# Router logits of a decoder block with the router's weights as the stationary operand, in two column halves that one further product adds and turns back

## The chip, the cores and the metric

The kernel runs on one NeuronCore of a Trainium2 chip. The metric is the device time of one execution in microseconds (us). Engines are called as the profile calls them: PE is TensorE's matmul, PEld its weight load, DVE VectorE, ACT ScalarE, POOL GpSimd, SP SyncE, whose queue issues most DMAs.

## The reference, cut to what matters

One decoder layer on 1024 tokens of width 1024: adaLN, one input projection, sliding-window attention beside a gated MLP, a merge, a residual, a second adaLN, and a mixture of 32 experts in 4 groups of 8. The change sits in the router of that mixture:

```python
hf = h.reshape(T, D)                                   # T = 1024 tokens, D = 1024
lg = (hf @ w_rg).astype(jnp.float32) + b_rg            # 4 group logits
g_idx = jnp.argmax(lg, axis=-1)                        # best group
le = ((hf @ w_re).astype(jnp.float32) + b_re).reshape(T, N_GROUPS, EXPERTS_PER_GROUP)
le = jnp.take_along_axis(le, g_idx[:, None, None], axis=1)[:, 0]
top_p, top_i = lax.top_k(jax.nn.softmax(le, axis=-1), TOP_K)   # two experts of that group
...
out = jax.ops.segment_sum(yr * row_w[:, None], row_tok, num_segments=T)   # experts on gathered tokens
```

## The kernel before, in words

The program has two parts. The first works on two halves of 512 tokens (`half(0)`, `half(1)`): projections, attention, the gated MLP and the merge, and after each half the product with `w_o` (`wo_stream(0)`, then `wo_pass` for the second half), which makes the residual `X1`. Nearly every large product there is three matmuls (`mm3`, L135 to L137): weights and activations are split into a rounded high part (cast on ACT, L451) and the rest (subtraction on DVE, L452). The second part runs the experts: their weights (2 MB each, `big` tiles, seven buffers) stream from HBM by SP's queue (L1391), and small expert blocks multiply 32 or 64 token columns as stationary operand (L1504).

The router stands between the parts. It works on eight tiles of 128 tokens, t = 0 to 7, with 40 columns of weights `wr` (4 groups, 4 unused, 32 experts):

- `r_setup` (L845) folds the modulation into `wr` (L850) and the bias `brt`.
- `r_pre` (L864, POOL) and `r_store` (L924 on DVE, L925 and L926 as POOL's DMAs) make the normalized tile and write it to HBM, from where the experts gather rows.
- `r_tr` (L852) transposes the tile in eight matmuls (L857) into two PSUM banks, and ACT copies each half to `h2T` (L858).
- `r_logit` (L872) multiplies: for each of eight blocks k of the contraction, the stationary operand is `h2T[:, k]` (128 x 128) and the moving one `wr[:, k]` (128 x 40); the sum stands in one bank `ps`, tokens on partitions (L876). Each such f32 matmul is two PE instructions and two loads in the trace. DVE then finds the best group and the two best experts (L878 to L897).
- `r_rank` (L900) counts, with three small matmuls (L903 to L906), how many earlier tokens chose the same expert; the last of them waits for DVE's choice `Mb` (L896). `tab_tok` (L942) makes from it the list of tokens, and from that POOL gathers the first expert's rows (L1416).

Tiles 0 to 3 are hooked into the jobs of `half(1)` (L1276), tiles 4 to 7 into the last pass of `w_o` (L1325, L1327). Within a queue the order is not the source's: the scheduler of the framework lays out each engine's instructions when the kernel is built, and each engine then works its list in order, waiting at the head. PSUM has eight banks in one pool (`bank()`); four of them hold the query sums of `half(1)` while tiles 0 to 3 pass.

Of the kernel before, what the change touches and what calls it, by code (L numbers as in the profile page):

```python
# [10 lines left out]
F32 = mybir.dt.float32  # L11
# [5 lines left out]
OP = mybir.AluOpType  # L17
AX = mybir.AxisListType

P = 128  # L20
# [81 lines left out]
def block_kernel(ctx: ExitStack, tc: tile.TileContext, x, c, positions, rel_bias, w_ada, b_ada,  # L102
# [6 lines left out]
    PE, DVE, ACT, POOL, SP = nc.tensor, nc.vector, nc.scalar, nc.gpsimd, nc.sync  # L109
# [11 lines left out]
    def nm(s):  # L121
        uid[0] += 1
        return f"{s}_{uid[0]}"
# [4 lines left out]
    def bank(shape=(512,)):  # L128
        return psum.tile([P] + list(shape), F32, name=nm("ps"), tag="ps")
# [17 lines left out]
    ident = keep.tile([P, P], F32, name="ident")  # L147
# [66 lines left out]
    pc = p1.enter_context(tc.tile_pool(name="p1c", bufs=1))  # L214
    hl = p1.enter_context(tc.tile_pool(name="p1hl", bufs=4))
    xw = p1.enter_context(tc.tile_pool(name="p1xw", bufs=5))
    sm = p1.enter_context(tc.tile_pool(name="p1sm", bufs=2))
# [604 lines left out]
        return j  # L822


    wr = pc.tile([P, 8, 40], F32, name="wr")
    brt = pc.tile([P, 40], F32, name="brt")
    sh2c = pc.tile([P, 8], F32, name="sh2c")
    g2c = pc.tile([P, 8], F32, name="g2c")
    DVE.memset(wr[:, :, 4:8], 0.0)
    DVE.memset(brt[:, 4:8], NEG)  # L830
    cum = keep.tile([P, 2, NE], BF16, name="cum")

# [12 lines left out]
    def r_setup():  # L845
        ps = bank()
        for k in range(8):
            PE.matmul(ps[:, 0:40], sh2c[:, k:k + 1].to_broadcast([P, P]), wr[:, k], start=(k == 0), stop=(k == 7))
        DVE.tensor_tensor(brt, ps[:, 0:40], brt, op=OP.add)
        DVE.tensor_tensor(wr, wr, g2c.unsqueeze(2).to_broadcast([P, 8, 40]), op=OP.mult)  # L850

    def r_tr(t, n):  # L852
        if n == 0:
# [17 lines left out]

    def r_logit(t):  # L872
        h2T = R.pop(("T", t))
        ps = bank()
        for k in range(8):
            PE.matmul(ps[:, 0:40], h2T[:, k], wr[:, k], start=(k == 0), stop=(k == 7))  # L876
        lg = sm.tile([P, 40], F32, name=nm("lg"), tag="lg")
        DVE.scalar_tensor_tensor(lg, ps[:, 0:40], R["rs", t], brt, op0=OP.mult, op1=OP.add)  # L878
        gm = sm.tile([P, 8], F32, name=nm("gm"), tag="gm")
        gi = sm.tile([P, 8], U32, name=nm("gi"), tag="gi")  # L880
        DVE.max(gm, lg[:, 0:8])
        DVE.max_index(gi, gm, lg[:, 0:8])
        pen = sm.tile([P, 4], F32, name=nm("pen"), tag="pen")
        DVE.tensor_tensor(pen, iota_u[:, 0:4], gi[:, 0:1].to_broadcast([P, 4]), op=OP.not_equal)
        le = sm.tile([P, 4, 8], F32, name=nm("le"), tag="le")
        DVE.scalar_tensor_tensor(le, pen.unsqueeze(2).to_broadcast([P, 4, 8]), NEG,
                                 lg[:, 8:40].rearrange("p (g e) -> p g e", g=4), op0=OP.mult, op1=OP.add)
        lef = le.rearrange("p a b -> p (a b)")
        ei = sm.tile([P, 8], U32, name=nm("ei"), tag="ei")
        DVE.max(mx8[:, t], lef)  # L890
        DVE.max_index(ei, mx8[:, t], lef)
        oh = sm.tile([P, 2, NE], F32, name=nm("oh"), tag="oh")
        DVE.tensor_tensor(oh, iota_u.unsqueeze(1).to_broadcast([P, 2, NE]),
                          ei[:, 0:2].unsqueeze(2).to_broadcast([P, 2, NE]), op=OP.is_equal)
        Mb = sm.tile([P, NE], BF16, name=nm("Mb"), tag="Mb")
        DVE.tensor_tensor(Mb, oh[:, 0], oh[:, 1], op=OP.add)  # L896
        DVE.tensor_scalar(lgs[:, t], lg[:, 0:4], gm[:, 0:1], None, op0=OP.subtract)  # L897
        R["oh", t] = (oh, Mb)
# [277 lines left out]
    def wo_stream(h):  # L1176
# [7 lines left out]
        for n in range(2):  # L1184
# [24 lines left out]
            jobs.hook(idx[-1], ev)  # L1209
            jm = jobs.add(*m)  # L1210
        jobs.hook(jm, lambda: (rows_load((1, 2)), r_setup()))
        return idx

# [60 lines left out]
    for t in range(4):  # L1274
        both = lambda fn: lambda t: (fn(t, 0), fn(t, 1))
        for d, fn in ((0, both(r_pre)), (0, r_sq), (0, both(r_tr)), (1, r_store), (2, r_logit), (4, r_rank)):  # L1276
            jobs.hook(q0 + 2 * t + d, lambda fn=fn, t=t: fn(t))
# [46 lines left out]
    for i, at in ((4, (1, 2, 4, 5, 7)), (5, (2, 3, 5, 6, 8))):  # L1324
        for j, fn in zip(at, (lambda t: r_tr(t, 1), r_logit, r_rank, tab_tok, r_store)):  # L1325
            jobs.hook(w2[j], lambda fn=fn, i=i: fn(i))
    for fn in (lambda t: r_tr(t, 1), r_store, r_logit, r_rank, tab_tok):  # L1327
        for i in (6, 7):
            jobs.hook(w2[-1], lambda fn=fn, i=i: fn(i))
# [439 lines left out]
    def table(t, cols, n):  # L1769
        if t == 0:  # L1770
            R["rest"] = bank()
        ps = R["rest"][:, 0:2 * n]
        tmp = wk.tile([P, D], F32, name=nm("y"), tag="y")
        A, C = (tmp[:, o:o + 2 * m].rearrange("p (k r) -> p k r", k=2) for o, m in ((0, P), (2 * P, n)))
        V = tmp[:, HT:HT + 4 * n].rearrange("p (k a n) -> p k a n", k=2, a=2)
        one_hots(A, C, t, cols)
        POOL.tensor_tensor(V[:, :, 0], C, wts[:, t].unsqueeze(2).to_broadcast([P, 2, n]), op=OP.mult)
        POOL.tensor_tensor(V[:, :, 1], C, pay[:, t].unsqueeze(2).to_broadcast([P, 2, n]), op=OP.mult)
        for k in range(2):
            PE.matmul(ps, A[:, k], V[:, k].rearrange("p a b -> p (a b)"), start=(t == 0 and k == 0),  # L1780
                      stop=(t == 7 and k == 1))
        return ps.rearrange("p (a n) -> p a n", a=2)
# [141 lines left out]
    with tc.If(nover > 0):  # L1924
# [32 lines left out]
        for t in range(8):  # L1957
            ps = table(t, cols[:, 0:NO], NO)
# [4 lines left out]
        with tc.For_i(0, nover, 1) as s:  # L1963
# [15 lines left out]
            for z, key in ((0, "g"), (1, "u")):  # L1979
                PS[X, key] = bank()  # L1980
                for kk in range(0, 8, 2):
                    wh, wl = split2(raws[z][:, kk:kk + 2])
                    for q in range(2):
                        k = kk + q
# [31 lines left out]
def build(inputs):  # L2016
    import concourse.bacc as _bacc

    nc = _bacc.Bacc("TRN2", target_bir_lowering=False, num_devices=1)
    arrays, args = {}, []  # L2020
    for name in _INS:
        a = np.ascontiguousarray(inputs[name])
        arrays[f"in_{name}_dram"] = a
        args.append(nc.dram_tensor(f"in_{name}_dram", a.shape, mybir.dt.from_np(a.dtype), kind="ExternalInput").ap())
    for i, (shape, dtype) in enumerate(_OUTS):
        dt = mybir.dt.from_np(np.dtype(dtype))
        args.append(nc.dram_tensor(f"out_{i}_dram", shape, dt, kind="ExternalOutput").ap())
    with tile.TileContext(nc) as tc:
        block_kernel(tc, *args)
    return nc, arrays  # L2030
# [8 lines left out]
```

## Time and profile before

| | us |
|---|---|
| median of 3 runs | 1276.06 (1275.82 to 1279.53) |
| the profiled execution | 1274.85 |
| its span, first to last instruction | 1273.2 |
| PE busy in the span | 1147.2 (90%) |
| DVE busy | 772.3 (61%) |
| ACT busy | 555.3 (44%) |
| POOL busy | 221.0 (17%) |
| mean granted clock of TensorE | 0.951 |

All sums below are made against the profiled execution; 1274.85 lies 1.21 under the median. Times within the program are us from the span's start. Busy shares are averages over stages with different limits, so the stretches around the router are what to read. A granted clock of 1.00 is 2.4 GHz, 0.50 is 1.2 GHz.

### The profile page before, as it was taken

How to read it: one execution, taken by the hardware profiler on the slowest of the kernel's cores; microseconds unless marked ns; L12 is line 12 of the kernel's file. 1: busy time of each engine (PE TensorE's matmuls, PEld its weight loads, DVE VectorE, ACT ScalarE, POOL GpSimd, SP SyncE). 2: the span in 40 equal slices, each digit the busy share in tenths (PEclk: the TensorE clock that was granted, in tenths of full speed). 3: DMA queues.
4: the chain of work that ended last, by engine and by line, in shares of the span. 5: the costliest groups of instructions: out<-in, count | busy, mean ns of one | idle time of the engine just before them, and what ended most of it. 6: DMA issues, size and time to landing. Idle time of an engine off the chain costs nothing. (4 is left out here: it accounts for less than half of the span.)

```text
span 1273.2 us, 18583 instructions
## 1 busy us (share of the span) xinstructions
PE 1147.2 (90%) x6873; PEld 878.1 (69%) x6874; DVE 772.3 (61%) x1698; ACT 555.3 (44%) x970; POOL 221.0 (17%) x325
## 2 busy tenths in 40 slices
PE   5899999999989999899996998998999998899851
PEld 3788887778878988688774665665665656676530
DVE  7668885567767888444497455664425635695015
ACT  4459742335525784233242244543414424673021
POOL 3500010111041000010034211121022121112201
PEclk9999999999989999899995999899999998999975
DMA  9734436547354345523856999999889999999994
GB/s 318 227 103 125 133 114 217 182 158 255 114 185 150 124 133 182 170 85 106 350 200 215 409 401 415 402 381 402 330 299 405 380 324 411 414 360 363 401 409 162
DMA packets 106345, 334.70 MB, mean 263 GB/s; under 512 B 7998, under 2 KB 52158, under 8 KB 81800
## 3 DMA queue, kind: packets, MB, share of 16 engines
q1 hardware_dynamic: 92438, 296.66, 61.6%
q0 software_dynamic: 13712, 36.77, 10.0%
q8 instruction: 55, 0.90, 0.3%
q14 instruction: 42, 0.34, 0.1%
q10 hardware_dynamic: 98, 0.03, 0.0%
HBM read 314.54 MB, written 25.71 MB: 267 GB/s over the span
## 5 line engine op out<-in xcount | busy, mean ns | idle before, releaser
L135 PE MATMUL ps<-big,hi 128*128 128x512 f32 x544 | 220.2, 405 | 9.7 <-ACT hi L451 9.4
L452 DVE TENSOR_TENSOR lo<-big,hi 128x1024 fp32r<-128x1024 f32 x156 | 185.5, 1221 | 67.1 <-ACT hi L451 66.3
L136 PE MATMUL ps<-big,hi 128*128 128x512 f32 x544 | 216.5, 398 | 4.1 <-DVE big L452 4.0
L137 PE MATMUL ps<-big,lo 128*128 128x512 f32 x544 | 215.7, 397 | 0.0
L451 ACT CAST hi<-st 128x512 fp32r<-128x512 f32 x192 | 116.2, 619 | 205.7 <-PE ps L136 117.4
L452 DVE TENSOR_TENSOR lo<-st,hi 128x512 fp32r<-128x512 f32 x192 | 135.3, 715 | 107.1 <-ACT hi L451 106.6
L451 ACT CAST hi<-big 128x1024 fp32r<-128x1024 f32 x156 | 159.4, 1050 | 69.1 <-PE ps L137 68.5
L1504 PE MATMUL ps<-big,xTh 128*32 128x128 f32 (+1 forms) x1792 | 133.4, 337 | 8.0 <-DMA big<-in_w_gate_dram 3.3
L135 PEld LDWEIGHTS ps<-big,hi 128*128 128x128 f32 x544 | 105.0, 193 | 33.4 <-ACT hi L451 11.1
L136 PEld LDWEIGHTS ps<-big,hi 128*128 128x128 f32 x544 | 104.9, 193 | 29.1 <-DVE big L452 5.9
L137 PEld LDWEIGHTS ps<-big,lo 128*128 128x128 f32 x544 | 104.5, 192 | 23.1 <-DVE lo L452 0.9
L1504 PEld LDWEIGHTS ps<-big,xTh 128*32 128x32 f32 (+1 forms) x1792 | 83.3, 126 | 48.7 <-issue 17.1
L136 PE MATMUL ps<-lo,xTh 128*128 128x512 f32 x224 | 94.2, 420 | 12.8 <-DVE lo L452 12.6
L135 PE MATMUL ps<-hi,xTh 128*128 128x512 f32 x224 | 94.2, 421 | 11.2 <-ACT hi L451 11.2
L137 PE MATMUL ps<-hi,xTl 128*128 128x512 f32 x224 | 91.3, 408 | 0.0
L135 PE MATMUL ps<-hi,big 128*128 128x256 f32 (+1 forms) x256 | 88.4, 346 | 0.1
L136 PE MATMUL ps<-lo,big 128*128 128x256 f32 (+1 forms) x256 | 86.8, 339 | 1.1 <-DVE lo L452 1.1
L137 PE MATMUL ps<-hi,big 128*128 128x256 f32 (+1 forms) x256 | 86.5, 338 | 0.0
L1421 POOL DMA_INDIRECT zd<-y,rows_i x30 | 50.8, 1695 | 175.3 <-DVE y L1581 96.1
L1416 POOL DMA_INDIRECT xg<-h2d,rows_i x30 | 36.2, 1207 | 220.9 <-PE ps L1448 101.5
L1504 PE MATMUL ps<-big,aTh 128*32 128x256 f32 (+1 forms) x448 | 64.3, 513 | 5.4 <-DMA big<-in_w_down_dram 5.4
L1577 DVE SCALAR_TENSOR_TENSOR y<-ps,w_sb,g 128x512 f32<-128x512 f32 (+1 forms) x20 | 12.9, 643 | 91.1 <-PE ps L1504 84.0
(382 smaller groups left out, 1865.5 us busy)
## 6 DMA issues: line engine op xcount, KB each, us to landing
big<-in_w_gate_dram SPq DMA_DIRECT2D x32, 2048.0 KB
big<-in_w_up_dram SPq DMA_DIRECT2D x32, 2048.0 KB
big<-in_w_down_dram SPq DMA_DIRECT2D x30, 2048.0 KB
st<-in_w_in_dram SPq DMA_DIRECT2D x26, 1024.0 KB
st<-in_w_ada_dram SPq DMA_DIRECT2D x16, 1024.0 KB
st<-in_w_o_dram SPq DMA_DIRECT2D x10, 1024.0 KB
big<-in_x_dram SPq DMA_DIRECT2D x16, 512.0 KB
bias<-biasd POOLq DMA_DIRECT2D x16, 512.0 KB
```

The costliest lines, as they stand in the source:

```text
L135: PE.matmul(ps, lh, rh, start=start, stop=False)
L136: PE.matmul(ps, lh, rl, start=False, stop=False)
L137: PE.matmul(ps, ll, rh, start=False, stop=stop)
L451: ACT.copy(hi, src)
L452: return DVE.tensor_tensor(lo, src, f(hi), op=OP.subtract)
L1416: return POOL.indirect_dma_start(out=t[0:n, 0:D // q], out_offset=None, in_=in_parts(src, q), in_offset=bass.IndirectOffsetOnAxis(ap=idx[0 ...
L1421: return POOL.indirect_dma_start(out=in_parts(dst, q), out_offset=bass.IndirectOffsetOnAxis(ap=idx, axis=0), in_=t[:, 0:D // q], in_offset ...
L1504: PE.matmul(ps[n * e:n * e + n, 0:m], xt[:, s * i:s * i + n], cols_w, start=start, stop=stop)
L1577: DVE.scalar_tensor_tensor(y, ps[:, 0:D // q], w, G2p[q], op0=OP.mult, op1=OP.mult)
```

## The change

`wr` gets 64 columns instead of 40, the last 24 of them zero. For block k the stationary operand is now `wr[:, k]` (128 x 64), the moving one `h2T[:, k]` (128 x 128 tokens). Even blocks sum into partitions 0 to 63 of a bank `pt`, odd ones into 64 to 127, so that matmuls of the two column halves of the array alternate. ACT copies the bank to `lT` (L882 of the changed kernel), and one more product (L884) with `f40`, two stacked 40-column identities, adds the halves and brings tokens back to partitions. `lT` takes its buffers from the tag `tA` of `tab_tok`, and each tile now takes two banks.

```diff
-    wr = pc.tile([P, 8, 40], F32, name="wr")
+    wr = pc.tile([P, 8, 64], F32, name="wr")
...
     DVE.memset(wr[:, :, 4:8], 0.0)
+    DVE.memset(wr[:, :, 40:64], 0.0)
+    f40 = pc.tile([P, 40], F32, name="f40")
+    DVE.tensor_tensor(f40, ident[:, 0:40], ident[:, 64:104], op=OP.add)
...
-            PE.matmul(ps[:, 0:40], sh2c[:, k:k + 1].to_broadcast([P, P]), wr[:, k], start=(k == 0), stop=(k == 7))
+            PE.matmul(ps[:, 0:40], sh2c[:, k:k + 1].to_broadcast([P, P]), wr[:, k, 0:40], start=(k == 0), stop=(k == 7))
         DVE.tensor_tensor(brt, ps[:, 0:40], brt, op=OP.add)
-        DVE.tensor_tensor(wr, wr, g2c.unsqueeze(2).to_broadcast([P, 8, 40]), op=OP.mult)
+        DVE.tensor_tensor(wr, wr, g2c.unsqueeze(2).to_broadcast([P, 8, 64]), op=OP.mult)
...
     def r_logit(t):
         h2T = R.pop(("T", t))
+
+        pt, lT = bank(), sm.tile([P, P], F32, name=nm("lT"), tag="tA")
+        for k in range(0, 8, 2):
+            for h in range(2):
+                PE.matmul(pt[64 * h:64 * h + 64, 0:P], wr[:, k + h], h2T[:, k + h], start=(k == 0), stop=(k == 6))
+        ACT.copy(lT, pt[:, 0:P])
         ps = bank()
-        for k in range(8):
-            PE.matmul(ps[:, 0:40], h2T[:, k], wr[:, k], start=(k == 0), stop=(k == 7))
+        PE.matmul(ps[:, 0:40], lT, f40, start=True, stop=True)
```

Lines after the edit move by 3 to 8: L857 becomes L860, L864 L867, L903 to L906 become L911 to L914, L925 becomes L933.

The scheduler also lays out other instructions anew. On PE at tiles 1 and 2, before (`ps_4408` is tile 1's logits, `ps_4452` and `ps_4458` are tile 2's transposes, `ps_4396` is tile 0's rank):

```order
L876 MATMUL ps_4408<-wr,h2T_4346 128x40 x4
L857 MATMUL ps_4452<-ident,big_3718 128x128
L876 MATMUL ps_4408<-wr,h2T_4346 128x40 x4
L857 MATMUL ps_4452<-ident,big_3718 128x128 x3
L857 MATMUL ps_4458<-ident,big_3718 128x128 x4
L135 MATMUL ps_4223<-big_3781,hi_4287 128x512
...
L135 MATMUL ps_4224<-big_3781,hi_4287 128x512
L906 LDWEIGHTS tri_b
L906 MATMUL ps_4396<-Mb_4327,tri_b 128x32
```

The same place now (`ps_4415` and `ps_4426` are tile 1's two products, `ps_4463` and `ps_4469` tile 2's transposes, `ps_4403` tile 0's rank):

```order
L881 MATMUL ps_4415<-h2T_4353,wr 64x128 x8
L137 MATMUL ps_4226<-big_3784,lo_4291 128x512
L135 MATMUL ps_4227<-big_3784,hi_4290 128x512
L884 MATMUL ps_4426<-f_187,lT_4416 128x40
L860 MATMUL ps_4463<-ident,big_3721 128x128
L914 LDWEIGHTS tri_b
L914 MATMUL ps_4403<-Mb_4334,tri_b 128x32
L860 MATMUL ps_4463<-ident,big_3721 128x128 x3
L860 MATMUL ps_4469<-ident,big_3721 128x128 x4
L136 MATMUL ps_4227<-big_3785,hi_4290 128x512
```

The rank product of tile 0 now stands after one of tile 2's eight transposes instead of after all eight; the number of 512-column matmuls ahead of it is the same (eight since tile 0's logits began to be due), and fourteen follow it before the next rank product in either order.

On POOL around the same tiles, before (`h_548` to `h_616` are tiles 0 to 3):

```order
L864 TENSOR_TENSOR h_548_4237<-big_3718,rc_4204 128x512 x2
L864 TENSOR_TENSOR h_568_4330<-big_3718,rc_4204 128x512 x2
L864 TENSOR_TENSOR h_592_4435<-big_3718,rc_4204 128x512
L925 DMA h2d<-h_548_4237 128x1024
L925 DMA h2d<-h_568_4330 128x1024
L864 TENSOR_TENSOR h_592_4435<-big_3718,rc_4204 128x512
L864 TENSOR_TENSOR h_616_4541<-big_3718,rc_4204 128x512 x2
```

And now:

```order
L867 TENSOR_TENSOR h_548_4240<-big_3721,rc_4207 128x512 x2
L867 TENSOR_TENSOR h_570_4337<-big_3721,rc_4207 128x512 x2
L933 DMA h2d<-h_548_4240 128x1024
L933 DMA h2d<-h_570_4337 128x1024
L867 TENSOR_TENSOR h_596_4446<-big_3721,rc_4207 128x512 x2
L867 TENSOR_TENSOR h_622_4556<-big_3721,rc_4207 128x512 x2
```

The fifth of the eight multiplications moved behind the two DMAs, so four stand in a row there instead of three.

On PE at the end of the router, tiles 6 and 7, before:

```order
L857 MATMUL ps_7281<-ident,big_6663 128x128 x4
L876 MATMUL ps_7293<-wr,h2T_7143 128x40 x8
L876 MATMUL ps_7320<-wr,h2T_7202 128x40 x8
L903 LDWEIGHTS ones_b
L903 MATMUL ps_7347<-ebase,ones_b 128x32
```

And now:

```order
L860 MATMUL ps_7308<-ident,big_6682 128x128 x4
L881 MATMUL ps_7320<-h2T_7170,wr 64x128 x8
L884 MATMUL ps_7331<-f_187,lT_7321 128x40
L881 MATMUL ps_7351<-h2T_7229,wr 64x128 x8
L884 MATMUL ps_7362<-f_187,lT_7352 128x40
L911 LDWEIGHTS ones_b
```

Each turning product follows its own tile's logits directly, with nothing between the two.

## Rows read from the trace of the kernel before

**Rows 1.** Busy time by stretch (us from the span's start). Columns: stretch, its length, then busy us and instruction count of PE, PEld, DVE, ACT and POOL, the granted clock, the DMA engines' busy share, GB/s.
```profile
340.00:400.00 60.00, 56.02 (x292) 47.35 (x291) 43.91 (x159) 20.11 (x38) 18.59 (x21) 0.91 0.48 160
368.00:373.00 5.00, 5.00 (x25) 5.00 (x26) 3.66 (x6) 0.57 (x1) 4.12 (x5) 0.50 0.37 147
400.00:520.00 120.00, 117.50 (x688) 103.05 (x686) 95.66 (x291) 75.67 (x175) 9.13 (x19) 1.00 0.47 153
640.00:671.00 31.00, 27.81 (x157) 21.64 (x156) 29.22 (x97) 12.99 (x28) 10.35 (x12) 1.00 0.64 228
671.00:690.00 19.00, 10.74 (x59) 9.88 (x59) 17.00 (x101) 3.53 (x7) 7.41 (x12) 0.50 0.75 265
690.00:700.00 10.00, 9.36 (x89) 5.37 (x93) 4.61 (x20) 3.80 (x6) 5.20 (x12) 0.50 0.35 105
700.00:980.00 280.00, 260.24 (x1607) 176.84 (x1598) 139.31 (x183) 106.72 (x139) 51.35 (x47) 0.98 0.98 382
```

**Rows 2.** All instructions of the logits' line: duration of one in ns (least, median, most), start of the first and the last, form.
```profile
L876 PEld LDWEIGHTS ps<-wr,h2T x128: 187/192/370, 362.5 to 678.3; 128*128 128x128 f32 x128
L876 PE MATMUL ps<-wr,h2T x128: 197/283/415, 362.7 to 678.3; 128*128 128x40 f32 x128
```

**Rows 3.** Order of time on PE and PEld around tile 5's logits: start, us taken by the row, engine, line, operation, count.
```profile
655.33 0.40 PE L137 MATMUL ps<-hi,big 128*128 128x512 f32 x1
655.33 1.99 PEld L876 LDWEIGHTS ps<-wr,h2T 128*128 128x128 f32 x16
655.56 1.87 PE L876 MATMUL ps<-wr,h2T 128*128 128x40 f32 x16
657.26 0.47 PE L135 MATMUL ps<-hi,big 128*128 128x512 f32 x1
```

**Rows 4.** The same view in the experts' part, where the stationary operand has 64 columns (`128*64`) or 32: full-width loads ahead of 64-column ones, those, and a full-width load after 32-column matmuls.
```profile
752.47 1.15 PEld L1458 LDWEIGHTS ps<-ident,xg 128*128 128x128 f32 x8
753.74 3.22 PEld L1504 LDWEIGHTS ps<-big,xTh 128*64 128x64 f32 x32
753.74 3.67 PE L1504 MATMUL ps<-big,xTh 128*64 128x256 f32 x32
703.50 0.14 PEld L1552 LDWEIGHTS ps<-ident,sl 128*128 128x128 f32 x1 [0.20 <-issue]
```

**Rows 5.** A matmul, ACT's copy of its result, and a load that waits for such a copy (order of time; in brackets the idle time before, and what ended it).
```profile
703.50 0.33 PE L1552 MATMUL ps<-ident,sl 128*128 128x128 f32 x1
703.86 0.27 ACT L1554 COPY aTh<-ps 128x128 f32<-128x128 f32 x1 [4.03 <-PE ps L1552]
690.01 0.59 ACT L1449 COPY xTh<-ps 128x512 f32<-128x512 f32 x1 [1.78 <-PE ps L1448]
690.64 1.48 PEld L1504 LDWEIGHTS ps<-big,xTh 128*32 128x32 f32 x32 [1.12 <-ACT xTh L1449]
```

**Rows 6.** PE in order of time at tiles 1 and 2.
```profile
365.46 0.50 PE L137 MATMUL ps<-big,lo 128*128 128x512 f32 x1
367.95 1.90 PE L876 MATMUL ps<-wr,h2T 128*128 128x40 f32 x8 [1.99 <-DVE lg L878]
371.46 1.74 PE L857 MATMUL ps<-ident,big 128*128 128x128 f32 x7
377.28 0.18 PE L906 MATMUL ps<-Mb,tri_b 128*128 128x32 bf16 x1 [1.99 <-DVE Mb L896]
377.31 0.59 PE L136 MATMUL ps<-big,hi 128*128 128x512 f32 x1
382.28 0.18 PE L903 MATMUL ps<-ebase,ones_b 1*128 1x32 bf16 x1
```

**Rows 7.** DVE and POOL in order of time at the same tiles.
```profile
368.80 2.27 DVE L924 SCALAR_TENSOR_TENSOR h<-h,rs,rb 128x1024 f32<-128x1024 f32 x1 [0.99 <-POOL h L864]
372.02 3.70 DVE L897 TENSOR_SCALAR lgs<-lg,gm 128x4 f32<-128x4 f32 x1
377.05 0.18 DVE L896 TENSOR_TENSOR Mb<-oh 128x32 bf16<-128x32 f32 x1
364.05 5.94 POOL L864 TENSOR_TENSOR h<-big,rc 128x512 f32<-128x512 f32 x4
371.93 3.75 POOL L864 TENSOR_TENSOR h<-big,rc 128x512 f32<-128x512 f32 x3
```

**Rows 8.** The end of the router in order of time: logits of tiles 6 and 7 on PE, their first reader on DVE (tile 7's), a DVE row beside POOL's memsets, the list of tokens, and the next weight load of SP's queue after 667.8.
```profile
671.86 6.89 PE L876 MATMUL ps<-wr,h2T 128*128 128x40 f32 x32
678.79 0.26 DVE L878 SCALAR_TENSOR_TENSOR lg<-ps,rs,brt 128x40 f32<-128x40 f32 x1 [0.62 <-PE ps L876]
680.43 1.30 POOL L1657 MEMSET z<- 128x512 f32 x4
680.64 1.11 DVE L913 CAST si<-sf 128x2 int32<-128x2 f32 x1
684.81 0.16 DVE L939 SCALAR_TENSOR_TENSOR tok_s<-tS,tk 128x4 int32<-128x4 f32 x1
698.21 0.38 SPq L1391 DMA_DIRECT2D big<-in_w_up_dram  x1
```

**Rows 9.** The scaling of `wr` in `r_setup`, and DVE's first wait of the program.
```profile
L850 DVE TENSOR_TENSOR wr<-wr,g2c x1: 482/482/482, 350.3 to 350.3; 128x320 f32<-128x320 f32 x1
7.09 0.21 DVE L313 COPY ccol<-ps 128x48 f32<-128x48 f32 x1 [3.93 <-PE ps L312]
```

## The prediction

> **What bounds the kernel now.** I read the busy time by stretch first, because the change touches two short windows. It shows [rows 1] three regimes. From 400 to 520, PE is busy 117.50 of 120 us: work taken from PE, or put on it, before that moves everything behind it. From 640 to 671, DVE is busy 29.22 of 31 and PE 27.81, so there DVE sets the pace. From 671 to 690 the clock is 0.50, PE is mostly idle, and a chain runs through PE and DVE to the list of tokens. From 700 on, the DMA engines are busy 0.98 of the time at 382 GB/s: the experts' part is a stream of weights. That stream stands at 0.35 between 690 and 700, since its buffers come free only when the first expert has multiplied; SP issues the next load at 698.21 [rows 8]. So the experts' end moves with the end of the router nearly one for one. The second view is order of time in the two windows. At tiles 1 and 2 it shows PE waiting twice, 1.99 us for tile 0's reader of the logits and 1.99 for tile 0's `Mb` [rows 6]; both times DVE is late because POOL multiplies beside it: L897 took 3.70 us, and it began and ended with POOL's three L864 [rows 7]. At tiles 6 and 7, PE does the logits in one piece of 6.89 us from 671.86, and DVE waits 0.62 for the last [rows 8].
>
> **What a tile's logits cost, before and after.** Before: 128 matmuls in eight tiles are 16 each [rows 2]. Tile 5's sixteen start at 655.56 and the next matmul starts at 657.26: 1.70 us, 0.106 each [rows 3]. A 40-column matmul is not what takes that long; the loads of 128 columns come at this pace (16 in 1.99 with the last one's length) [rows 3]. At the low clock it is 6.89/32 = 0.215 [rows 8].
>
> After: a load has 64 columns, a matmul 128 moving columns. The nearest rows are the experts' with 64-column stationary operands and 256 moving ones: 32 in 3.67 us, and less the last one's overhang of about 0.25 that is 0.107 each, while 32 loads take 3.22 [rows 4]. Half the moving columns make 0.053, and loads of 64 at half the pace of 128 [rows 3] are 0.053 too. Sixteen take 0.86 at the full clock, 1.72 at the low one. The bounds are 0.053 and the 0.106 of now; I take the lower since those rows have the same pattern of halves. The Trainium skill (TensorE: Matmul & The Clock Gate, Part 3: Packing small matmuls) has a rule against this: a load overlaps matmuls in flight only where the row groups differ, and here only column groups differ. By that rule a tile would cost 16 x (0.053 + 0.107) = 2.56, by the rows 0.86; the rows bear against it, since 64-column loads and matmuls run side by side there [rows 4].
>
> Going into and out of the half-width form costs something: a full-width load after narrow matmuls stood idle 0.20 [rows 4], and the first 64-column load starts at 753.74, 0.12 after the last full-width one ended (752.47 + 1.15), with its matmul at the same instant instead of 0.23 behind [rows 3, 4]. I take 0.2 each way, 0.4 a tile (0 to 0.6). The turning product is two more full-width loads, 0.21 (0.43 at the low clock). So a tile at the full clock goes from 1.70 to 0.86 + 0.4 + 0.21 = 1.47: **0.23 less**, not the half that the columns suggest.
>
> The product waits for ACT's copy. From a 128-column matmul's start to the copy is 0.36, of which 0.11 is its own columns; the copy takes 0.27; a load follows a copy's end by 0.04 [rows 5]. That is 0.25 + 0.27 + 0.04 = 0.56. At tiles 0 to 5, two or three 512-column matmuls (0.23 each, 655.33 to 655.56 [rows 3]) stand between, 0.45 and more, and with the change of form (0.2) that covers it. At tiles 6 and 7 nothing stands between and the wait is bare.
>
> **The sum.** *Tiles 0 and 1* gain nothing: PE waits behind them for DVE anyway, and tile 1's product waits for tile 0's reader as its logits did. *Tiles 2 to 5*: 4 x 0.23 = -0.9, but the new order breaks into the logits of tiles 2 and 4 with another matmul, two more changes there and back, +0.8; together **-0.1** (-3.8 if all of tiles 0 to 5 kept 0.63 each, with no change of form; +1.5 if each product waits 0.4). *Tile 0's rank product* now stands ahead of seven transposes of tile 2. `Mb` comes when POOL lets DVE go: before, POOL's last three ended at 375.68 and `Mb` came at 377.05 [rows 7]. Now four stand in a row, but can start earlier, since L924 of tile 1, at 368.80, no longer runs beside a fifth (2.27 us with it) [rows 7]; the one makes up for the other and I keep 377.3. The seven transposes, formerly done before the wait, come after it: 1.74 at the low clock, some 1.5 at the 0.215 pace. The fourteen matmuls after them, 4.97 us from 377.31 to 382.28 [rows 6], then start later and more of them at the full clock, 0.7 back: **+0.8** (-0.3 to +3.4). *Tiles 6 and 7*: each 0.2 + 1.72 + 0.56 + 0.43 = 2.91, together 5.8 against 6.7 (6.89 less the last one's overhang): **-0.9** (-2.0 to +1.0). *DVE's chain* then reaches the rank of tile 7 earlier against POOL's memsets at 680.43, beside which L913 took 1.11 [rows 8]; it may slip past: **-0.5** (-1.0 to 0).
>
> Edits without a price: the wider memset and `f40` fall into DVE's wait of 3.93 before 7.09; were it gone, they are a few tenths. The scaling of 512 instead of 320 elements is 0.48 x 1.6 = 0.77 instead of 0.48 [rows 9], 0.3 on a DVE that is busy 43.91 of 60 there [rows 1]; uncovered it would be +0.3. `lT` shares its two buffers with `tab_tok`, whose earlier users are done when it is written. Eight copies of 0.27 are 2.2 us on ACT, busy 20.11 of 60 and 12.99 of 31 [rows 1].
>
> Sum: -0.1 + 0.8 - 0.9 - 0.5 = -0.7. Against the profiled 1274.85 that is 1274.2; the median stands 1.21 above it, so I forecast **1275.4 against 1276.06: no change**. A measurement of this kernel can tell about 0.3%, 3.8 us, from no change.
>
> **Rivals.** *Faster.* The change of form costs nothing, the product is always covered and tiles 0 and 1 keep their share: 6 x 0.63 = 3.8, -2.0 at the end and -1.0 at the memsets make 1276.1 - 6.8 = 1269.3. For it: PE is the bound after 400 [rows 1]. Against it: the 0.20 rows, and the two waits for DVE that swallow what tiles 0 and 1 save [rows 4, 6].
>
> *Slower, by the rank product.* Place: tile 0's rank on PE. If POOL's four multiplications hold DVE for all of 5.94 us (four before [rows 7]) from about 370.4, `Mb` comes 0.7 later; the transposes add 1.5; and with PE standing some 7 us the low clock, which came after a wait of 1.99 before [rows 1, 6], may hold for all fourteen matmuls, six more of them at twice their time, +1.2. That is +3.4, 1279.5, the gain at the end being lost where DVE sets the pace. It decides from the point where `Mb` comes after 377.3. Against it: POOL's start is set by DVE's L924, which now runs alone.
>
> *Slower, because the halves take turns.* The change would then not do what it says. With load and matmul one after the other a tile costs 2.56 instead of 0.86: 6 x (1.70 - 0.23) + 2 x (3.4 - 0.45) = +14.7, 1290.8. It decides from a pace of 0.10 per matmul. Against it: 0.107 with twice the columns [rows 4]. The Trainium skill's rule above is this case.
>
> **How the numbers follow.** The forecast case has 0.74, the faster rival 0.12 (two thirds of it, 0.08, beyond 3.8 us), the rank product 0.11 (half of it beyond), the turns 0.03. Inside the forecast case I leave 0.04 beyond 3.8 us on either side, since in both windows POOL, DVE and the clock act on each other and the order is laid out anew. So: faster by over 0.3% 0.08 + 0.04 = 0.12, slower 0.055 + 0.03 + 0.035 = 0.12, within 0.76. The likeliest time is 1275.4. The range takes in the terms' bounds on the likely side of both rivals, 1271.5 to 1280.0, and leaves the ends of the faster rival and the turns out.
>
> **What would show it.** In the changed profile: 64-column logits at 0.05 to 0.06 each at the full clock (0.107 means turns); PEld idle about 0.2 before and after them; the product of tiles 6 and 7 waiting some 0.5 for ACT; 6.0 us instead of 6.9 from the first logits of tile 6 (671.86 before) to tile 7's reader (678.79 before) [rows 8]; PE waiting once for long, about 6 us, at tile 0's rank; SP's first load after the router within 2 us of 698.2. The forecast is wrong if the stretch 340 to 400 changes by over 3 us, or if the experts' stream changes its length rather than its start.

## The result, and the profile after

The changed kernel takes **1285.49 us** (median of 4 runs, 1285.22 to 1289.44), the kernel before 1276.18 beside it: ratio **1.0076 (95% interval 1.0055 to 1.0097)**, 9.3 us slower. The forecast was 1275.4 in a range to 1280.0. It was wrong. The first profiled execution (1289.44) lies 4 us above the other three runs; so the rows of after are those of a second one, at 1285.50 (e4_after_again below, span 1283.8). Line numbers are 3 to 8 higher than before: the logits are L881, the copy L882, the turning product L884, its reader L886, `Mb` L904, the rank product L911 to L914, SP's loads L1399.

Busy time by stretch of after, as [rows 1] (us, then PE, PEld, DVE, ACT, POOL, granted clock, DMA share, GB/s):

```profile
340.00:400.00 60.00, 51.69 (x288) 41.26 (x287) 41.86 (x133) 21.18 (x43) 16.95 (x18) 0.91 0.44 150
400.00:520.00 120.00, 120.00 (x694) 103.72 (x694) 97.78 (x313) 75.87 (x175) 10.64 (x21) 1.00 0.45 147
640.00:671.00 31.00, 30.88 (x166) 23.94 (x165) 24.89 (x54) 15.22 (x33) 10.10 (x9) 1.00 0.67 251
671.00:690.00 19.00, 12.58 (x88) 9.00 (x87) 16.82 (x85) 4.36 (x10) 5.36 (x8) 0.87 0.56 205
700.00:980.00 280.00, 260.26 (x1652) 177.86 (x1653) 141.50 (x209) 106.86 (x139) 54.50 (x57) 0.97 0.96 372
```

The stretches hold a little other work than before, since all comes 4 to 11 us later; but where PE was busy 117.50 of 120 it is now busy throughout. The logits did become shorter: tile 5 on PE and its weight loads, as [rows 3]:

```profile
665.98 0.39 PE L137 MATMUL ps<-hi,big 128*128 128x512 f32 x1
666.30 1.09 PE L881 MATMUL ps<-h2T,wr 128*64 128x128 f32 x16
667.33 0.50 PE L135 MATMUL ps<-hi,big 128*128 128x512 f32 x1
667.66 0.40 PE L136 MATMUL ps<-lo,big 128*128 128x512 f32 x1
667.89 0.31 PE L884 MATMUL ps<-f,lT 128*128 128x40 f32 x2
668.03 0.48 PE L137 MATMUL ps<-hi,big 128*128 128x512 f32 x1
668.35 0.39 PE L135 MATMUL ps<-hi,big 128*128 128x512 f32 x1
```

```profile
666.30 0.85 PEld L881 LDWEIGHTS ps<-h2T,wr 128*64 128x64 f32 x16 [0.36 <-issue]
667.32 0.19 PEld L135 LDWEIGHTS ps<-hi,big 128*128 128x128 f32 x1 [0.17 <-issue]
```

From 665.98 to 668.35 there are four 512-column matmuls, 0.93 us at their pace here of 0.233; the rest, 1.44, is the tile. Before it was 1.70 from the logits' first start to the next matmul's [rows 3]. That next matmul too was followed late, 0.32 after its start and not 0.227 (before, PE):

```profile
657.58 0.39 PE L136 MATMUL ps<-lo,big 128*128 128x512 f32 x1
```

Counted like the 1.44, from 655.33 [rows 3] to 657.58 less two at 0.227, the tile took 1.80.

Tiles 1 and 2 on PE, as [rows 6], then the DVE and POOL rows that hold `Mb` back, as [rows 7]:

```profile
371.50 1.09 PE L881 MATMUL ps<-h2T,wr 128*64 128x128 f32 x16
375.09 0.39 PE L884 MATMUL ps<-f,lT 128*128 128x40 f32 x2 [1.83 <-DVE lg L886]
381.98 0.19 PE L914 MATMUL ps<-Mb,tri_b 128*128 128x32 bf16 x1 [6.37 <-DVE Mb L904]
382.00 1.74 PE L860 MATMUL ps<-ident,big 128*128 128x128 f32 x7
388.89 0.18 PE L911 MATMUL ps<-ebase,ones_b 1*128 1x32 bf16 x1
```

```profile
375.34 5.24 DVE L905 TENSOR_SCALAR lgs<-lg,gm 128x4 f32<-128x4 f32 x1
381.74 0.19 DVE L904 TENSOR_TENSOR Mb<-oh 128x32 bf16<-128x32 f32 x1
```

```profile
375.63 4.91 POOL L867 TENSOR_TENSOR h<-big,rc 128x512 f32<-128x512 f32 x4
```

And the end of the router, as [rows 8], on PE, DVE, POOL and SP:

```profile
683.57 1.09 PE L881 MATMUL ps<-h2T,wr 128*64 128x128 f32 x16
685.09 0.41 PE L884 MATMUL ps<-f,lT 128*128 128x40 f32 x2 [0.42 <-ACT lT L882]
686.95 0.41 PE L884 MATMUL ps<-f,lT 128*128 128x40 f32 x2 [0.42 <-ACT lT L882]
687.29 0.18 PE L911 MATMUL ps<-ebase,ones_b 1*128 1x32 bf16 x1
```

```profile
688.33 1.28 DVE L932 SCALAR_TENSOR_TENSOR h<-h,rs,rb 128x1024 f32<-128x1024 f32 x1
689.70 0.24 DVE L886 SCALAR_TENSOR_TENSOR lg<-ps,rs,brt 128x40 f32<-128x40 f32 x1
692.74 1.71 DVE L921 CAST si<-sf 128x2 int32<-128x2 f32 x1
```

```profile
692.61 0.53 POOL L1391 DMA_DIRECT2D big<-in_w_down_dram  x1 [2.17 <-PE ps L914]
693.13 1.30 POOL L1665 MEMSET z<- 128x512 f32 x4
697.39 1.11 POOL L1424 DMA_INDIRECT xg<-h2d,tok_s  x1 [2.96 <-DVE ol L1705]
```

```profile
709.22 0.38 SPq L1399 DMA_DIRECT2D big<-in_w_up_dram  x1
```

The clock under those products (us, PE, clock, DMA share, GB/s) was the full one, not the 0.50 of before [rows 1]:

```profile
683.50:687.30 3.80, 2.96 (x39) 1.00 0.99 393
```

None of these places holds 9 us. A stretch with nothing of the router in it does: the split products of the weights (L135 to L137, 512 columns), ten steps from start to start, before and then after, from PE's timeline:

```profile
579.69 0.39 PE L136 MATMUL ps<-big,hi 128*128 128x512 f32 x1
...
581.96 0.39 PE L137 MATMUL ps<-big,lo 128*128 128x512 f32 x1
```

```profile
579.63 0.39 PE L136 MATMUL ps<-big,hi 128*128 128x512 f32 x1
...
581.96 0.40 PE L137 MATMUL ps<-big,lo 128*128 128x512 f32 x1
```

Before, ten steps take 2.27 us, **0.227 each**; after 2.33, **0.233 each**, at a granted clock of 1.00 both times. The mean over some 1500 such pairs up to 700 us, with `big` as the moving operand and `hi` or `lo` as the stationary one, is 0.2273 and 0.2333. The experts' 512-column matmuls, behind 700, keep their pace (0.2315 before and 0.2316 after, over some 800 pairs at the full clock), so it isn't the clock nor the execution. What differs ahead of 700 is the memory, by the addresses in the two built programs: `wr` takes 768 more bytes of a partition and `f40` 160, and the pools behind them, with `hi` and `lo` of the split weights (p1hl), start at 163392 in place of 162464. The other operand, in big, stays at 21408.

### The profile page after: what moved, and what is told of

It reads as the page before. It is cut to its first block, busy times and chain, and to the rows that moved or that the text cites. A ratio compares the mean times of both kernels' runs of the same rounds, so it can differ in the third digit from the quotient of the medians.

```text
span 1287.8 us, 18634 instructions
## 1 busy us (share of the span) xinstructions
PE 1158.8 (90%) x6889; PEld 873.1 (68%) x6890; DVE 776.1 (60%) x1700; ACT 557.2 (43%) x978; POOL 216.8 (17%) x325
## 5 line engine op out<-in xcount | busy, mean ns | idle before, releaser
L135 PE MATMUL ps<-big,hi 128*128 128x512 f32 x544 | 221.1, 406 | 8.5 <-ACT hi L451 8.1
L137 PE MATMUL ps<-big,lo 128*128 128x512 f32 x544 | 219.4, 404 | 0.0
L135 PEld LDWEIGHTS ps<-big,hi 128*128 128x128 f32 x544 | 104.5, 192 | 34.8 <-ACT hi L451 9.9
L137 PEld LDWEIGHTS ps<-big,lo 128*128 128x128 f32 x544 | 104.2, 192 | 25.7 <-DVE lo L452 1.1
L135 PE MATMUL ps<-hi,xTh 128*128 128x512 f32 x224 | 94.7, 424 | 11.2 <-ACT hi L451 11.2
L137 PE MATMUL ps<-hi,xTl 128*128 128x512 f32 x224 | 91.6, 409 | 0.0
L135 PE MATMUL ps<-hi,big 128*128 128x256 f32 (+1 forms) x256 | 88.9, 348 | 0.0
L137 PE MATMUL ps<-hi,big 128*128 128x256 f32 (+1 forms) x256 | 86.7, 339 | 0.0
```

Source lines behind the costliest of these rows:

```text
L135: PE.matmul(ps, lh, rh, start=start, stop=False)
L137: PE.matmul(ps, ll, rh, start=False, stop=stop)
```

## The experiments

Each edit that moves a pool allocates bytes that nothing uses; the order of instructions on every engine stays that of the kernel it starts from. Ratios are to the kernel before, timed beside it. "Apart" is the start of p1hl less that of big, modulo 256; "pace" the mean above; the interval is of 95%.

| run | p1hl moved by | apart | pace, us | median, us | ratio to before |
|---|---|---|---|---|---|
| before | 0 | 0 | 0.2273 | 1274.85 to 1276.93 | 1 |
| e1_before_pad928 | 928 | 160 | 0.2333 | 1283.15 | 1.0057 (1.0036 to 1.0078) |
| e2_before_pad32 | 32 | 32 | 0.2333 | 1281.18 | 1.0045 (1.0027 to 1.0062) |
| f1_before_hl32 | 32 | 32 | 0.2332 | 1279.93 | 1.0026 (1.0006 to 1.0045) |
| g3_before_pad96 | 96 | 96 | 0.2341 | 1281.86 | 1.0057 (1.0035 to 1.0080) |
| g4_before_pad128 | 128 | 128 | 0.2324 | 1281.91 | 1.0042 (1.0018 to 1.0066) |
| i1_before_pad256 | 256 | 0 | 0.2273 | 1277.19 | 1.0010 (0.9995 to 1.0026) |
| i2_before_pad512 | 512 | 0 | 0.2274 | 1276.35 | 1.0005 (0.9988 to 1.0022) |
| f2_before_all32 | 32, big too | 0 | 0.2274 | 1277.36 | 0.9996 (0.9978 to 1.0013) |
| e4_after_again | 928 | 160 | 0.2333 | 1284.10 | 1.0066 (1.0047 to 1.0085) |
| f3_after_pad32 | 960 | 192 | 0.2295 | 1279.27 | 1.0009 (0.9987 to 1.0032) |
| e3_after_pad96 | 1024 | 0 | 0.2274 | 1277.41 | 1.0021 (1.0004 to 1.0037) |
| g2_after_pad96_again | 1024 | 0 | 0.2273 | 1278.65 | 1.0026 (1.0004 to 1.0047) |

**The place, not the order.** e1, e2 and e3 add to the allocation of `g2c`, in before (232 and 8 floats) and in the change (24); e4 is the change unaltered:

```diff
-    g2c = pc.tile([P, 8], F32, name="g2c")
+    g2c = pc.tile([P, 8], F32, name="g2c"); pad = pc.tile([P, 232], F32, name="pad")
```

e1: 

> The kernel before, with 928 unused bytes per partition allocated behind g2c: as many as the change's wider wr (768) and f40 (160) take, so that the pools behind it (p1hl, p1xw, p1sm) lie where the change puts them; the order of instructions is that of before. Theory PLACE (the 1.1 us per 120 us and more that the 512-column matmuls of the first 700 us lost, 0.2333 us from one to the next in place of 0.2267 to 0.2275, come from where their operands lie): the pace is 0.233 here too, 2080 such matmuls x 0.0055 = up to 11 us, less what waits swallow: 1283 to 1287 us. Theory ORDER (the loss comes from tile 0's rank product ahead of seven transposes and from the new order behind it): 1276 +- 1, pace 0.227. A third, EXECUTION (the profiled execution of the change only happened to run slowly): 1276 and 0.227 here as well.

e2: 

> The kernel before, with 32 unused bytes per partition behind g2c: the pools behind it move from addresses that are 32 past a multiple of 64 to multiples of 64, as with 928 bytes, and hardly anywhere else. PLACE, if the remainder by 64 is what counts: pace 0.233 and 1283 to 1287 us as in e1_before_pad928; PLACE, if some larger stride counts: between 1276 and 1287, unlike e1. ORDER and EXECUTION: 1276 +- 1.

e3: 

> The changed kernel with 96 more unused bytes per partition behind g2c, so that the pools behind it stand 1024 bytes from where they were before and the remainder by 64 is 32 again; order of instructions as in the change. PLACE: pace 0.227 again, and the time of the change without its displacement: 1275 to 1278 us, by the prediction's terms 1275.4, by the 2 us that tile 0's rank cost 1277. ORDER: 1285.5 as the change, pace whatever it is. EXECUTION: 1285.5 in the median.

e4: 

> The changed kernel unaltered. All theories: 1285.5 us. PLACE: its profiled execution shows 0.233 us from one 512-column matmul to the next before 700 us, and the same pace as before behind 708, where the pools have been laid out anew. EXECUTION: 0.227 in a profile at 1285.5.

PE's timeline of e1, and then of e3, nine steps each:

```profile
579.67 0.39 PE L136 MATMUL ps<-big,hi 128*128 128x512 f32 x1
...
581.77 0.39 PE L136 MATMUL ps<-big,hi 128*128 128x512 f32 x1
```

```profile
579.82 0.39 PE L135 MATMUL ps<-big,hi 128*128 128x512 f32 x1
...
581.86 0.39 PE L135 MATMUL ps<-big,hi 128*128 128x512 f32 x1
```

2.10 us in the old kernel that was moved, 2.04 in the changed one that was moved back: 0.233 and 0.227. PLACE held in all four, in the pace exactly; ORDER and EXECUTION fell. The times follow, though e2's 1281.18 stayed below the 1283 it expected at least: the displacement alone costs 7.3 us (0.57%, 4.6 to 9.9), and taking it out of the change gives back 5.7 (0.66% to 0.21%).

**Which pool, and by which stride.** f1 pads p1hl itself, and p1xw once more; f2 pads in keep, ahead of big; f3, g3, g4, i1 and i2 are the first edit with 8 (on the change), 24, 32, 64 and 128 floats.

```diff
# f1
+    pad = hl.tile([P, 8], F32, name="pad", bufs=1); padx = xw.tile([P, 8], F32, name="padx", bufs=1)
# f2
-    prow_i = keep.tile([P, 2], I32, name="prow_i")
+    prow_i = keep.tile([P, 2], I32, name="prow_i"); pad = keep.tile([P, 8], F32, name="pad")
```

f1: 

> The kernel before; pool p1hl (the halves hi and lo of the split weights) alone moves by 32 bytes, p1xw and p1sm behind it by 64, p1c and big not at all. If the place of p1hl sets the pace of the 512-column matmuls: 0.233 us from one to the next and 1281 to 1283 us, as with e2_before_pad32. If it is that of p1xw or p1sm (the state of the tokens, small tiles, the buffers that DVE and ACT write beside the matmuls): 0.227 and 1275 to 1276.

f2: 

> The kernel before; every pool from big on moves by 32 bytes, so that both operands of the matmuls (hi or lo in p1hl, the other one in big) stand at multiples of 64. If the pace hangs on where p1hl lies by itself: 0.233 and 1281 to 1283 us. If it hangs on whether the two operands have the same remainder by 64 (before: 32 and 32; after: 32 and 0): 0.227 and 1275 to 1276.

f3: 

> The changed kernel with 32 more unused bytes behind g2c: p1hl, p1xw and p1sm lie 960 bytes from where they were before, again 32 past a multiple of 64, but not at the same remainder by 512 as in e3_after_pad96 (1024 bytes). If the remainder by 64 is all that counts: pace 0.227 and 1277 us as in e3; if a larger stride counts: between that and 1284.

g3: 

> The kernel before with p1hl, p1xw and p1sm moved by 96 bytes: the two operands lie 96 apart by 128, in place of 0 before, 32 in the change and e1 to f1, and 64 in f3. If any remainder but 0 costs: pace of 512-column matmuls 0.229 to 0.234 and 1279 to 1283 us; if 96 is as good as 0: 0.227 and before's time.

g4: 

> The kernel before with the three pools moved by 128 bytes. If the pace goes by the distance of the operands modulo 128: 0.227 and before's time. If it goes by 256 or more (before, e3 and f2 have the same remainder by 256 too): a slower pace and up to 1283 us.

i1: 

> The kernel before with p1hl, p1xw and p1sm moved by 256 bytes. 128 bytes cost the pace (g4: 0.232), 1024 did not (e3, g2: 0.227). If the distance of the two operands counts modulo 256: 0.227 and before's time. If modulo 512 or 1024: 0.232 to 0.234 and 1280 to 1283 us.

i2: 

> The kernel before with the three pools moved by 512 bytes. If the distance counts modulo 256 or 512: 0.227 and before's time. If modulo 1024: 0.232 to 0.234 and 1280 to 1283 us.

PE's timeline of f1, and then of f2, nine steps each, 2.10 and 2.04 us:

```profile
579.78 0.40 PE L135 MATMUL ps<-big,hi 128*128 128x512 f32 x1
...
581.88 0.40 PE L135 MATMUL ps<-big,hi 128*128 128x512 f32 x1
```

```profile
579.44 0.39 PE L135 MATMUL ps<-big,hi 128*128 128x512 f32 x1
...
581.48 0.39 PE L135 MATMUL ps<-big,hi 128*128 128x512 f32 x1
```

p1hl 32 bytes further, with big in its place, slows the pace; big moved along restores it. So p1hl's own address doesn't count, but its distance to something that f2 moves along: big, the matmul's other operand, or one of the pools between them (p1st, p1c), which f2 moves as well. A second pair of operands points to the matmul's own two: L681 and L682 multiply a tile of p1sm with big, f1 moves p1sm by 64 and e2 by 32, and their pace (some 45 pairs each) is 0.2300 in f1 and 0.2335 in e2, while that of L135 to L137 is the same in both (before, 0.2286). The experts' operands, which by their addresses lie 32, 160 or 224 apart in before and after alike, never reach 0.2273 either: their groups run at 0.2290 to 0.2342 before. The remainder by 64, e2's idea, fell with f3 (960 bytes: 0.2295) and g4, though g3 would agree with it; by 256 every row of the table agrees. f1's time moved less (3.3 us, 0.8 to 5.7) than that of e2 at the same pace (5.7, 3.4 to 7.9), and missed its 1281 to 1283; the two intervals overlap, and what p1xw and p1sm, which f1 puts elsewhere than e2, add to it is open.

**What the change costs in its old place.** e3 and g2 are the same kernel, twice 2.7 and 3.3 us above before, where the prediction's terms gave -0.7. f4 and g1 hook the ranks of tiles 0 to 3 two jobs later (on the change moved by 960 and by 1024), h1 does so in the kernel before, h2 hooks them one job later:

```diff
-(2, r_logit), (4, r_rank)):
+(2, r_logit), (6, r_rank)):
```

f4: 

> f3_after_pad32 with the ranks of tiles 0 to 3 hooked two jobs later (6 for 4): on PE tile 0's rank product then stands behind tile 2's transposes and fourteen 512-column matmuls, where PE waited 6.4 us for Mb ahead of them. If that wait is PE's alone: 3 to 5 us less than f3, 1272 to 1274 us, and the wait is gone. If DVE and POOL set the pace there (the fourteen then wait for their banks), or the time is given back in the later stages: within 1 us of f3.

g1: 

> The change with both costs taken away: 96 unused bytes behind g2c, so that p1hl stands 1024 bytes from where it was before (same remainder by 128 as big), and the ranks of tiles 0 to 3 hooked two jobs later. If the place costs what e3 against e4 showed and the rank's wait 3 us as f4 against f3: 3 us below e3, 2 to 4 below before, 1272 to 1275 us. If the two share a cause, or the place only mattered together with the wait: within 1 us of before.

g2: 

> e3_after_pad96 once more, beside g1: the change without its displacement. The prediction's own terms (-0.7) give before -0.7; its two costs at tile 0 as e3's trace shows them, less the gain at the end, give -1 to +2; if something else of the change costs as much as e3's first median said, +2.6.

h1: 

> The kernel before with the ranks of tiles 0 to 3 hooked two jobs later, as in f4 and g1. If g1's 3.5 us against g2 only undo what the change had brought (PE's longer wait at tile 0's rank): before gains at most the 1.99 us that PE waits there for Mb, 0 to -2. If the later hook is a gain of its own, whatever the logits look like: -3 to -4 here too, and the change without its displacement costs some 2.8 us elsewhere.

h2: 

> g2_after_pad96_again with the ranks of tiles 0 to 3 hooked one job later (5 for 4): on PE the rank product of tile 0 then follows all of tile 2's transposes, as it did before the change, and two 512-column matmuls. If its place ahead of seven transposes is what the change loses: most of g1's gain, 1274 to 1276. If it is the wait for Mb itself, which only fourteen matmuls cover: within 1 us of g2, 1277 to 1279.

| run | median, us | ratio to before |
|---|---|---|
| f4_after_pad32_rank6 | 1276.09 | 0.9988 (0.9966 to 1.0009) |
| g1_after_pad96_rank6 | 1273.58 | 0.9992 (0.9974 to 1.0011) |
| h1_before_rank6 | 1274.20 | 0.9987 (0.9969 to 1.0005) |
| h2_after_pad96_rank5 | 1276.75 | 1.0003 (0.9981 to 1.0026) |
| h3_after_pad96_oldlogits | 1277.49 | 1.0010 (0.9987 to 1.0033) |
| h4_after_pad96_late | 1279.21 | 1.0022 (0.9999 to 1.0045) |

PE in e3, and its clock behind the wait in e3 and in g2 (us, PE, clock, DMA share, GB/s):

```profile
380.90 0.18 PE L914 MATMUL ps<-Mb,tri_b 128*128 128x32 bf16 x1 [6.37 <-DVE Mb L904]
386.41 0.18 PE L911 MATMUL ps<-ebase,ones_b 1*128 1x32 bf16 x1
```

```profile
383.00:385.00 2.00, 2.00 (x9) 0.79 0.00 0
```

```profile
381.00:383.00 2.00, 2.00 (x7) 0.50 0.00 0
383.00:385.00 2.00, 2.00 (x6) 0.52 0.70 264
```

After the same wait of 6.37, the clock was 0.50 to about 383.8 in e3 and to nearly 385 in g2, whose wait had ended 2 us earlier. In g1 the wait has shrunk, and in h1 from 1.99 (PE, one row of each):

```profile
379.29 0.18 PE L914 MATMUL ps<-Mb,tri_b 128*128 128x32 bf16 x1 [1.03 <-DVE Mb L904]
```

```profile
377.73 0.18 PE L906 MATMUL ps<-Mb,tri_b 128*128 128x32 bf16 x1 [0.92 <-DVE Mb L896]
```

By the ratios g1 is 4.3 us below g2 and f4 2.7 below f3 (3, and 3 to 5, were expected); but g1, expected 2 to 4 below before, is only 1.0 below it (between 3.3 gained and 1.4 lost). h1 gains 1.7 in the old kernel (0.13%, between 4.0 gained and 0.6 lost), within what its wait of 1.99 could give. So a part of the gain may be the later hook's own, and the rest undo the change's longer wait; h2, which only puts the rank behind the transposes again, is at before + 0.4, between its two expectations. The intervals, some 2 us each way, don't settle how it divides. No version is surely faster than before.

h3 keeps the setup edits with the old logits, h4 has the new logits in tiles 4 to 7 and the old ones in the others; both with p1hl moved by 1024. The core of h4 (h3 is its `else` for all tiles):

```diff
+        if t >= 4:
...
+        else:
+            ps = bank()
+            for k in range(8):
+                PE.matmul(ps[:, 0:40], h2T[:, k], wr[:, k, 0:40], start=(k == 0), stop=(k == 7))
```

h3: 

> Only the setup edits of the change: wr 64 wide with its memset, f40, the scaling of 512 elements in place of 320, and 96 unused bytes behind them (p1hl 1024 bytes from its old place); the logits are those of before, eight full-width matmuls a tile on wr's first 40 columns, no copy and no product. Prediction: these edits cost nothing, before +- 1 us. If the 2.8 us of e3 and g2 come from them: before + 2 to 3.

h4: 

> g2_after_pad96_again with the change's logits in tiles 4 to 7 alone; tiles 0 to 3 as before the change. Prediction's terms for tiles 4 to 7 and the end: -1.4 to -2 against before, 1273 to 1275. If the loss of e3 and g2 lies in tiles 4 to 7 or in the setup: before + 2 to 3; if in tiles 0 to 3: before or below it.

Both intervals hold zero, or touch it, and hold e3's 2.7 too (h3 +1.3, h4 +2.8): where the loss of e3 and g2 lies they don't decide. But h4 does rule out the gain of 1.4 to 2 that the prediction's terms gave for tiles 4 to 7, since at best it gains 0.1. In the traces neither loses anything at tile 0's rank: from L1112's start to the rank of tile 1 they are within 0.2 us of before.

## Why the prediction was wrong

**The step that failed** is "Edits without a price: the wider memset and `f40`". It priced them as work for DVE and not as memory. The 928 bytes shift p1hl against big, and 2016 matmuls of 512 columns (the groups of L135 to L137) that the diff doesn't name cost 0.006 more each: 12 us on PE, less 0.7 for 384 of 256 columns, which go from 0.1199 to 0.1179. Half of the 2016 run ahead of 345, and yet e1 is only 1.38 late there, so waits seem to swallow a part; 5.7 to 7.3 us reach the end. No rival was built on it, and the last sentence of the prediction, on when the forecast is wrong, looked at 340 to 400 and at the experts, not at 400 to 640, where it shows. Starts of the same instructions, before first, and what they are later by:

| | L1112, at 345 | rank of tile 1 | logits of tile 6 | SP's load L1391 | span |
|---|---|---|---|---|---|
| before | 345.01 | 382.28 | 671.86 | 698.21 | 1273.2 |
| e1, place alone | +1.38 | +1.57 | +6.01 | +6.22 | +10.0 |
| e3, change without place | +3.40 | +4.13 | +4.97 | +4.10 | +2.5 |
| g2, the same | +1.37 | +3.53 | +5.10 | +4.42 | +3.9 |
| e4, change | +4.40 | +6.61 | +11.71 | +11.01 | +10.6 |

Read the steps between columns, not the sums: up to 345 one execution differs from another by some us whatever the kernel, and the experts' stream by up to 6. From the rank of tile 1 to SP's load, place costs 4.65 and the change 4.40; without place the change costs -0.03 and 0.89.

Of the other steps some held, and some came out near by luck.

**The halves**: sixteen loads in 0.85 are 0.053 each, as taken; the rival of turns is dead (its 2.56 was also too high: it took 0.107 for a matmul that the same paragraph had put at 0.053, and 16 x (0.053 + 0.053) is 1.70). The change of form was put too high: the first of the sixteen matmuls comes 0.09 late and the sixteen take 1.03 in place of 0.86, 0.26 together and not 0.4; the 0.1 by which the second 512-column start behind them is late stood there before too. With the product a tile costs 1.44, forecast 1.47, but counted the same way it was 1.80 and not 1.70, so it gains 0.36, not 0.23. The Trainium skill (TensorE: Matmul & The Clock Gate, Part 3: Packing small matmuls) lets a load overlap only where row groups differ; here it overlaps between column halves, and the measurement decides.

**Tile 0's rank**: one wait of 6.37 (forecast about 6); `Mb` at 381.74, which is 377.3 and the 4.4 that all was late. L905 took 5.24 beside POOL's four multiplications, 1.5 longer than L897 [rows 7], but began 1.1 earlier by that clock. The step was 0.73 in e3, 2.21 in e4: forecast 0.8, up to 3.4. The difference is how long the low clock held behind the wait (e3 2.9 us, g2 and e4 6), the point of the second rival.

**Tiles 2 and 3**: from the rank of tile 1 to that of tile 3 e3 takes 16.08 us, as before (402.49 - 386.41 and 398.36 - 382.28 [rows 6]).

**Tiles 4 and 5** did not gain: from the rank of tile 1 to the first logits of tile 6, e3 takes 0.84 and g2 1.57 longer than before, and e4 0.66 longer than e1, where the forecast had -0.1 for tiles 2 to 5. (Five executions with the old logits and the old pace, before, f2, h3, i1 and i2, take 289.0 to 290.3 between the two points, e3 290.4 and g2 291.1.) In e3, g2 and e4 the clock fell to 0.50 once more for 3.4 us shortly ahead of tile 6 (e3 from 667.1), which it did not do before; what of the loss is that, and what the order, is not shown.

**Tiles 6 and 7**: 0.42 of waiting for ACT (forecast 0.5), 6.13 from the first logits to the last reader (forecast 6.0, before 6.9). That 6.0 was luck. In e4 the clock was 1.00 there, and PE was through in 3.72 (683.57 to 687.29) in place of the forecast 5.8; in e3, at 0.50, it took 5.45; the reader came after 6.13 and 6.14. So DVE sets it, whose L932 of 1.28 now stands right ahead of that reader, not PE's sum. And the gain of 0.8 did not pass on: POOL's memsets, which start 9.56 after the first logits in place of 8.57 [rows 8], now fall on tile 7's L921 and stretch it to 1.71, where they had fallen on tile 6's L913 (1.11); what holds POOL up there is open. From the first logits to the first gather it is 13.82, before 13.97: of -0.9 and -0.5, -0.15 is left. (From there to SP's load e3, g2 and e4 are another 0.54 faster, but so is g3 with the old logits, and h4 with the new ones is not.) One reading was wrong as well: from 671 to 690 PE was not mostly idle but busy 10.74 of 19 [rows 1]; no term hung on it.

So from L1112 to SP's load the rows give +0.7 (e3) and +3.05 (g2) for the change in its old place, and e4 1.77 more than e1, not -0.7; the timed 2.7 and 3.3, with lower ends at 0.5, hold all three. These are single executions of each kernel, so the sizes of the parts are rough.

## What to carry to other kernels

A wider constant is an edit of everything allocated behind it. Before pricing a diff that changes a tile's size, list the addresses of the operands of the busiest matmuls in both programs, and after it compare the pace of matmuls that the diff doesn't touch; if it moved, pad the tile so that the distance between the operands is a multiple of 256 bytes again, and only then judge the idea. A wait on PE can be shortened by what is queued ahead of it: the rank two jobs later took 5.3 of 6.4 us from it here (g1), though 2.3 came back at tile 3's transposes.

## What the runs showed of the hardware

The pace of fp32 matmuls of 512 columns depended on the distance between moving and stationary operand in SBUF modulo 256 bytes. With big moving and p1hl stationary it was 0.2273 at 0 (displacements 0, 256, 512, 1024, and both by 32), 0.2324 to 0.2341 at 32, 96, 128 and 160, 0.2295 at 192. In some 330 pairs of the same lines the roles are reversed, p1hl moving and big stationary: 0.2283 at 0, and 0.2328 to 0.2339 at the others, 192 included. Those of 256 columns, which have the reversed roles too, went the other way: 0.1199 at 0 and 96, 0.1179 at 160, 0.1151 at 192. Why is not shown; 64 and 224 weren't tried.
